# Moving a kernel's row loads behind its first tiles, and its first results into the last product

## The chip, the cores and the metric

The kernel runs on one core of a Trainium2 chip. Its engines are TensorE (PE in the profile), VectorE (DVE), ScalarE (ACT), GpSimd (POOL) and SyncE (SP); DMAs are issued from the queues of SyncE, ScalarE and GpSimd. The metric is the device time of one execution in microseconds, lower is better; of three runs of the kernel before the median counts. Beside them stands one profiled execution.

## The reference

One inference step of a hybrid decoder layer in float32, on 256 prompt tokens and on 8 samples of 8 tokens, 320 tokens in all, of width 2048:

```python
xn = rms_norm(x, g_mix)
z = xn @ w_in                  # [B | C | h | q | k | v | gate_conv | gate_attn]
u = c_gate * h_conv
y_conv = (b_gate * short_conv(u, w_conv)) @ w_conv_out      # causal, width 3
y_attn = window_attention(q, k, v, rel_bias, sinks) @ w_attn_out
merged = sigmoid(gate_c) * y_conv + sigmoid(gate_a) * y_attn
h = x + merged @ w_o
hn = rms_norm(h, g_ffn)
h = h + (silu(hn @ w_gate) * (hn @ w_up)) @ w_down          # inner width 5632
y = rms_norm(h, g_final)       # y_prompt (256 rows), y_sample (64 rows)
```

Returned are y for the prompt and the samples, and the new keys, values and convolution states.

## The kernel before, in words

Every product is computed in pieces of float32r: a loaded weight tile `wraw` is split into a high part `whi` (a copy on ScalarE, line 104) and a low part `wlo` (a subtraction on VectorE, line 105), and for each pair of tiles TensorE runs high by high, low by high and high by low. The rings hold four `wraw`, three `whi` and three `wlo`, so that loads and splits run ahead of TensorE by a few tiles. Weight loads are issued from SyncE's queue. The order of instructions on each engine is fixed when the program is built: a scheduler takes them in program order as far as, by its own model, they are ready; `after(...)` places an instruction behind another one of the same engine.

The start. `vecs` (line 199) holds the norm's weights. x comes in twice: transposed, as `hT` (`x_load`, line 259, the first chunk from ScalarE's queue and the others from SyncE's, six issues among the weight tiles by the table `XA`), and by rows, as `xr` (`row_load`, line 342, six loads from GpSimd's queue). The first product is `kv_product` (line 297) with nine weight tiles: two of one chunk of 128 rows, seven of two chunks. For each tile `x_prep` splits the chunks of `hT` into `xh_t` and `xl_t` (lines 272 and 273, both with `vecs`), then the weights are split and the matmuls of line 316 run, 12 for a chunk. After every tile `tick()` runs one step of the side work `start_rest` (line 349): it builds the bias table through the tile `e_sb`, then issues `row_load` 0 to 2 behind the fifth tile, 3 and 4 behind the sixth, and from the eighth tile on squares one row tile a step on ScalarE (`row_square`, line 347); `row_load(5)` stands behind the first square. The sums of these squares give the norm's root, which enters only when results are taken out of the product. Nothing holds a row load back, so the scheduler may issue it as soon as its buffer is free.

`at_pace` (line 154) is a mark: VectorE copies one element out of the last low part (`last["low"]`) into `marks` (line 157), and GpSimd copies it into `pace` (line 158); what is put behind that copy on GpSimd waits for the tile's split. Before, it is used in later stages alone, and `kv_product` does not set `last["low"]`.

The end. The last product, w_down, is computed by `down(g, ...)` (line 905) for two halves g of the output columns, as a seven-product scheme on sums of blocks; the products come in the order `ORDER`, and the last is `Q4`, of three weight tiles (six matmuls each) in the last piece. After a product `merge` adds the PSUM bank to the rows `hr` (tokens 0 to 127 and 128 to 255) and `done` takes the finished columns' squares (line 1003) into `ssf` and multiplies them by g_final (line 1006). The samples' sums `hs` are folded from two halves of the partitions by `sample_sum` (line 1013: four matmuls into `pz`, a square and a multiplication into `ysm`), which stands before the third tile of each Q4. `before_last` (line 1032), after the last matmul of the last Q4, finishes the first token tile (`finish`: root, two scalings, two stores of 512 KB from SyncE, line 1059) and takes the samples' root (a small matmul into `pzs`, line 1036). Then Q4 is merged into the second token tile (line 903), its last square and root are taken, and lines 1067 to 1081 scale it in four parts of 512 columns with a store each, and scale and store the samples (`ysm`) in two stores.

Of the kernel before, what the change touches and what calls it, by code (L numbers as in the profile page):

```python
# [44 lines left out]
def hybrid_layer(ctx: ExitStack, tc: tile.TileContext, a: dict, o: list):  # L45
# [27 lines left out]
    def after(*marks):  # L73

        es = ExitStack()
        for m in marks:
            es.enter_context(tc.issue_after(m.ins))
        return es
# [6 lines left out]
    def ring_tile(tag, shape, dt):  # L85
        extra = {"wraw": 2, "whi": 1, "wlo": 1}[tag]
        i = turn[tag]
        turn[tag] = (i + 1) % (ring[tag] + (extra if more else 0))
        if i >= ring[tag]:
            return more[0].tile(shape, dt, tag=tag, name=u(tag), bufs=extra)  # L90
        return wp.tile(shape, dt, tag=tag, name=u(tag), bufs=ring[tag])
# [62 lines left out]
    def at_pace():  # L154
        i = paced[0]
        paced[0] += 1
        nc.vector.tensor_copy(marks[:, i:i + 1], last["low"][0:1, 0, 0:1].bitcast(F32))  # L157
        return nc.gpsimd.tensor_copy(pace, marks[:, i:i + 1])  # L158
# [37 lines left out]
                nc.gpsimd.dma_start(flat(block(dst, g, i)), flat(block(src, g, i)))  # L196

    vecs = cst.tile([P, 56], F32, name="vecs")
    nc.gpsimd.dma_start(vecs, a["vecs"])
    ident = cst.tile([P, P], F32, name="ident")  # L200
    nc.gpsimd.memset(ident, 0.0)
    ident_in = nc.gpsimd.affine_select(
# [94 lines left out]
    def kv_product(tiles):  # L297
        ps = [ps_acc(u("kv")) for _ in range(4)]
        k0 = 0
        for i, n in enumerate(tiles):  # L300
            for k in range(k0, k0 + n):
                x_prep(k)
            raw = ring_tile("wraw", [P, 2, CK], F32)
            nc.sync.dma_start(raw[:, :n, :], a["w_kv"][:, k0:k0 + n, :])
            for c0, cn in XA.get(i, ()):
                x_load(c0, cn, nc.sync)
            hi, lo = ring_tile("whi", [P, 2, CK], F32R), ring_tile("wlo", [P, 2, CK], F32R)
            with after(*mark[k0 + n - 1]):
                split_to(hi[:, :n, :], lo[:, :n, :], raw[:, :n, :])
            order = [(k, c) for k in range(n) for c in range(4)]  # L310
            if k0 + n == KC:
                order.sort(key=lambda kc: kc[1])
            for k, c in order:
                kc = k0 + k
                for m, (w, x) in enumerate(((hi, xh), (hi, xl), (lo, xh))):
                    last["mm"] = nc.tensor.matmul(  # L316
                        ps[c][:, :T], w[:, k, c * P:(c + 1) * P], x(kc),
                        start=(kc == 0 and m == 0), stop=(kc == KC - 1 and m == 2),
                    )
            k0 += n  # L320
            tick()
        return ps
# [14 lines left out]
    def row_load(i):  # L337
        t, h = i // 2, i % 2
        t0, tn = TOK[t]
        tag, w = (("s", 1536), ("s", 1536), ("pT", 1536), ("bias", 1024), ("bias", 1024), ("s", 1536))[i]  # L340
        r = pr.tile([P, w], F32, tag=tag, name=u("xr"), bufs=1 if tag == "pT" else 2)
        nc.gpsimd.dma_start(r[:tn, 0:1024], a["x_rows"][t0:t0 + tn, h * 1024:(h + 1) * 1024])
        xr[i] = r[:tn, 0:1024]

    def row_square(i):
# [559 lines left out]
    def down(g, k0, nk, done):  # L905
        sa, al2 = made[0]
        samp = {}
        n1 = slice(g * 2 * SW, (g * 2 + 1) * SW)
        n2 = slice((g * 2 + 1) * SW, (g * 2 + 2) * SW)
        for prods in ORDER:  # L910
            bank = {prod: ps_acc(u(prod)) for prod in prods}
            for prod in prods:
                side = STREAMS[prod][2]
                if side and side not in samp:
                    samp[side] = ps_aux(u("n" + side))
            for i in range(nk // KP):
                if final[0] and prods == ("Q4",) and i == nk // KP - 1:
                    sample_sum(g, n1, n2)
                for prod in prods:
                    name, xv, side = STREAMS[prod]  # L920
                    v = A_OF[prod]
                    hi, lo = load_block(block(name, g, k0 // KP + i), [P, KP, SW])
                    for j in range(KP):
                        kk = i * KP + j
                        first, end = kk == 0, kk == nk - 1
                        xh_, xl_ = a_h[:, v, kk, :], a_l[:, v, kk, :] if v < 5 else al2[:, v - 5, kk, :]
                        for m, (x, w) in enumerate(((xh_, hi), (xl_, hi), (xh_, lo))):
                            last["mm"] = nc.tensor.matmul(  # L928
                                bank[prod], x, w[:, j, :],
                                start=(first and m == 0), stop=(end and m == 2),  # L930
                            )
                        if side:
                            for m, w in enumerate((hi, lo)):
                                last["mm"] = nc.tensor.matmul(  # L934
                                    samp[side], sa[:, xv, kk, :], w[:, j, :],
                                    start=(first and m == 0 and prod == SHARED[side][0]),
                                    stop=(end and m == 1 and prod == SHARED[side][1]),
                                )
                    while pending:
                        with after(last["lo"]):  # L940
                            pending.pop(0)()
                    tick()
            if final[0] and g == 1 and prods == ("Q4",):
                before_last(n2)
            for prod in prods:
                merge(prod, bank[prod], n1, n2)
                done(g, prod, n1, n2)
                side = STREAMS[prod][2]
                if side and prod == SHARED[side][1]:
                    ns = n1 if side == "a" else n2  # L950
                    nc.vector.tensor_add(hs[:, ns], hs[:, ns], samp[side])
                    done(g, "n" + side, n1, n2)
# [10 lines left out]
    for piece, nf in enumerate(PIECES):  # L963
# [41 lines left out]
        def scaled(y, ns):  # L1005
            nc.vector.tensor_mul(y[:, ns], y[:, ns], gfb[:y.shape[0], ns])
# [6 lines left out]
        def sample_sum(g, n1, n2):  # L1013
            pz = ps_aux(u("pz"))
            for h, ns in enumerate((n1, n2)):
                nc.tensor.matmul(
                    pz[h * 64:h * 64 + 64, :], sel[:, 0:64], hs[:, ns], start=True, stop=True
                )
            square(pz, ssf[:, 2, g:g + 1])
            nc.vector.tensor_mul(ysm[:, g, 0:SW], pz, ysm[:, g, SW:2 * SW])  # L1020

        def done(g, prod, n1, n2):
            if not final[0]:
                return
            for p, t, ns in (("P2", 0, n1), ("P7", 1, n2), ("Q3", 0, n2), ("Q4", 1, n1)):
                if p == prod:
                    c = ns.start // SW
                    square(hr[:, t, ns], ssf[:, t, c:c + 1])
                    if g == 0 or p in ("P2", "P7"):
                        scaled(hr[:, t, :], ns)  # L1030

        def before_last(n2):
            scaled(hr[:, 0, :], n2)
            finish(0, hr[:, 0, :], y_p[0, 0:P, :], P, nc.sync)
            pz = ps_aux("pzs")
            nc.tensor.matmul(pz[:, 0:2], sel, ssf[:, 2, 0:2], start=True, stop=True)
            nc.vector.tensor_copy(ssf[:, 2, 0:2], pz[:, 0:2])
            nc.vector.memset(ssf[:, 2, 2:4], 0.0)
            root(2)

        roots = {}

# [21 lines left out]
        side_work[0] = sum_work(2)  # L1064
        f0 += nf

    r = root(1)
    y, dst = hr[:, 1, :], y_p[0, P:TP, :]
    e = slice(2 * SW, 3 * SW)
    nc.vector.scalar_tensor_tensor(y[:, e], y[:, e], r, gfb[:, e], op0=ALU.mult, op1=ALU.mult)  # L1070
    nc.scalar.activation(y[:, 0:SW], y[:, 0:SW], AF.Copy, scale=r)
    nc.sync.dma_start(dst[:, e], y[:, e])
    nc.scalar.dma_start(dst[:, 0:SW], y[:, 0:SW])
    nc.vector.tensor_scalar(y[:, SW:2 * SW], y[:, SW:2 * SW], r, None, op0=ALU.mult)
    nc.vector.tensor_scalar(y[:, 3 * SW:D], y[:, 3 * SW:D], r, None, op0=ALU.mult)
    nc.sync.dma_start(dst[:, SW:2 * SW], y[:, SW:2 * SW])
    nc.scalar.dma_start(dst[:, 3 * SW:D], y[:, 3 * SW:D])
    ys = y_s.flatten_outer_dims().rearrange("t (g h n) -> t h g n", g=2, h=2)
    nc.scalar.activation(ysm[:, :, 0:SW], ysm[:, :, 0:SW], AF.Copy, scale=roots[2])
    for h, eng in ((0, nc.scalar), (1, nc.sync)):  # L1080
        eng.dma_start(ys[:, h], ysm[h * 64:h * 64 + 64, :, 0:SW])


_IN = ['x', 'w_kv', 'w_in', 'w_conv_out', 'w_attn_out', 'w_o', 'w_gate', 'w_up', 'w_down', 'vecs', 'state_conv',
# [84 lines left out]
```

## Time and profile before

| | |
|---|---|
| runs before | 1684.08, 1684.56, 1684.93 us (median 1684.56) |
| profiled execution | 1686.09 us, span 1684.1 us |
| granted TensorE clock | 0.996 mean |
| busy share PE, DVE, ACT, POOL | 99%, 58%, 43%, 12% |
| DMA | 388.31 MB, mean 231 GB/s |

The span reaches from the first to the last instruction of the profiled execution. Busy times are sums over an engine's instructions; an idle engine costs something only where the others wait for it. In the timeline a row has the start, the duration, the engine, the line and the operation, out and in; a trailing q marks the engine's queue, which issues DMAs. In the view by windows a row has the stretch, its length, the busy time of PE, PEld (weight loads of TensorE), DVE, ACT and POOL with the number of instructions, then the granted clock, the mean busy share of the DMA engines and GB/s.

### The profile page before, as it was taken

What the parts mean: (1) busy time and instruction counts of PE and PEld (TensorE: products, weight loads), DVE (VectorE), ACT (ScalarE), POOL (GpSimd) and SP (SyncE); (2) the same over time, 40 slices, a digit from 0 to 9 for tenths busy, and PEclk for the clock granted to TensorE, in tenths of its full rate; (3) what the DMA queues carried; (4) which work ended last, traced back from release to release, by engine and by line L of the source; (5) the groups of instructions that cost most, each with busy time, mean ns of one, the idle gap of its engine ahead of it and who ended that gap; (6) DMA issues with size and microseconds to landing.
All of it is one profiled execution on the core that took longest, in us unless ns stands there. A gap on an engine that the chain in (4) does not pass through costs nothing.

```text
span 1684.1 us, 26855 instructions
## 1 busy us (share of the span) xinstructions
PE 1664.7 (99%) x10692; PEld 1592.6 (95%) x10692; DVE 983.3 (58%) x1544; ACT 724.9 (43%) x934; POOL 200.6 (12%) x449
## 2 busy tenths in 40 slices
PE   8999999999999999999999999999999999999996
PEld 7999999999999999999999988899999888999975
DVE  5457645444444444446555577755555777555686
ACT  6345433333333334445333355433333554333464
POOL 2001211111111112211111100011111000110000
PEclk9999999999999999999999999999999999999998
DMA  9554545888888889997787878888877788787584
GB/s 302 178 145 121 178 137 155 279 256 240 249 246 250 252 252 293 291 282 224 219 225 227 226 244 267 268 251 227 222 225 216 241 274 268 232 233 202 192 280 153
DMA packets 91549, 388.31 MB, mean 231 GB/s; under 512 B 12320, under 2 KB 12640, under 8 KB 84224
## 3 DMA queue, kind: packets, MB, share of 16 engines
q1 hardware_dynamic: 78048, 282.20, 51.5%
q0 software_dynamic: 12800, 103.46, 25.1%
q8 instruction: 83, 1.36, 0.3%
q10 hardware_dynamic: 576, 0.95, 0.2%
q14 instruction: 42, 0.34, 0.1%
HBM read 383.32 MB, written 97.48 MB: 285 GB/s over the span
## 4 chain that ended last, share of the span: by engine, by line
PE 97%; DVE 1%; DMA 1%; ACT 0%; issue 0%; SPq 0%; DVEq 0%; ACTq 0%
PE fu L128 18%; PE fg L128 18%; PE P L928 7%; PE wo L128 7%; PE gc L128 7%; PE ga L128 7%; PE Q L928 5%; PE C L128 3%; PE yc L128 3%; PE ya L128 3%; PE B L128 3%; PE q L128 3%; PE H L128 3%; PE nb L934 2%; PE na L934 2%; PE kv L316 2%
## 5 line engine op out<-in xcount | busy, mean ns | idle before, releaser
L105 DVE TENSOR_TENSOR wlo<-wraw,whi 128x1024 fp32r<-128x1024 f32 (+1 forms) x531 | 650.3, 1225 | 579.1 <-ACT whi L104 576.8
L104 ACT ACTIVATE whi<-wraw 128x1024 fp32r<-128x1024 f32 (+1 forms) x531 | 562.0, 1059 | 790.3 <-PE fu L128 159.0
L128 PE MATMUL fu<-hh_t,whi 128*128 128x320 f32 x704 | 217.9, 309 | 0.0
L128 PE MATMUL fg<-hh_t,whi 128*128 128x320 f32 x704 | 217.8, 309 | 0.0
L128 PE MATMUL fu<-hl_t,whi 128*128 128x320 f32 x704 | 217.8, 309 | 0.0
L128 PE MATMUL fg<-hh_t,wlo 128*128 128x320 f32 x704 | 217.8, 309 | 0.0
L128 PE MATMUL fu<-hh_t,wlo 128*128 128x320 f32 x704 | 217.8, 309 | 0.0
L128 PE MATMUL fg<-hl_t,whi 128*128 128x320 f32 x704 | 217.7, 309 | 0.0
L158 POOL COPY pace<-marks 1x1 f32<-1x1 f32 x180 | 35.4, 196 | 1038.5 <-DVE marks L157 1038.4
L128 PEld LDWEIGHTS fg<-hh_t,whi 128*128 128x128 f32 x704 | 132.3, 188 | 0.1
L128 PEld LDWEIGHTS fg<-hl_t,whi 128*128 128x128 f32 x704 | 132.3, 188 | 0.1
L128 PEld LDWEIGHTS fu<-hh_t,whi 128*128 128x128 f32 x704 | 132.3, 188 | 0.1
L128 PEld LDWEIGHTS fu<-hl_t,whi 128*128 128x128 f32 x704 | 132.3, 188 | 0.0
L128 PEld LDWEIGHTS fu<-hh_t,wlo 128*128 128x128 f32 x704 | 132.3, 188 | 0.0
L128 PEld LDWEIGHTS fg<-hh_t,wlo 128*128 128x128 f32 x704 | 132.3, 188 | 0.0
L128 PE MATMUL wo<-m_h,whi 128*128 128x320 f32 x256 | 79.8, 312 | 0.0
L128 PE MATMUL wo<-m_h,wlo 128*128 128x320 f32 x256 | 79.3, 310 | 0.0
L128 PE MATMUL wo<-m_l,whi 128*128 128x320 f32 x256 | 79.2, 310 | 0.0
L128 PE MATMUL gc<-xh_t,wlo 128*128 128x320 f32 x256 | 79.1, 309 | 0.0
L128 PE MATMUL ga<-xl_t,whi 128*128 128x320 f32 x256 | 79.1, 309 | 0.0
L128 PE MATMUL gc<-xh_t,whi 128*128 128x320 f32 x256 | 79.1, 309 | 0.0
L128 PE MATMUL gc<-xl_t,whi 128*128 128x320 f32 x256 | 79.1, 309 | 0.0
(313 smaller groups left out, 3405.3 us busy)
## 6 DMA issues: line engine op xcount, KB each, us to landing
T<-in_w_down_dram POOLq DMA_DIRECT2D x132, 512.0 KB, 7.1
wraw<-in_w_in_dram SPq DMA_DIRECT2D x128, 512.0 KB, 4.2
wraw<-in_w_gate_dram SPq DMA_DIRECT2D x88, 512.0 KB, 4.7
wraw<-in_w_up_dram SPq DMA_DIRECT2D x88, 512.0 KB, 4.8
wraw<-T SPq DMA_DIRECT2D x88, 512.0 KB, 4.4
wraw<-in_w_down_dram SPq DMA_DIRECT2D x66, 512.0 KB, 4.4
T<-T POOLq DMA_DIRECT2D x44, 512.0 KB, 5.5
wraw<-in_w_o_dram SPq DMA_DIRECT2D x32, 512.0 KB, 6.8
```

The lines of the kernel that those rows point to most:

```text
L104: last["hi"] = nc.scalar.activation(hi, src, AF.Copy)
L105: last["lo"] = nc.vector.tensor_sub(lo, src, hi.bitcast(F32))
L128: last["mm"] = nc.tensor.matmul(ps[c][:, :T], w[:, k, c * P:(c + 1) * P], x(kc), start=(kc == 0 and i == 0), stop=(kc == nk - 1 and i == 2),)
L158: return nc.gpsimd.tensor_copy(pace, marks[:, i:i + 1])
L316: last["mm"] = nc.tensor.matmul(ps[c][:, :T], w[:, k, c * P:(c + 1) * P], x(kc), start=(kc == 0 and m == 0), stop=(kc == KC - 1 and m == 2),)
L928: last["mm"] = nc.tensor.matmul(bank[prod], x, w[:, j, :], start=(first and m == 0), stop=(end and m == 2),)
L934: last["mm"] = nc.tensor.matmul(samp[side], sa[:, xv, kk, :], w[:, j, :], start=(first and m == 0 and prod == SHARED[side][0]), stop=(end ...
```

## The change

- `vecs` is loaded from ScalarE's queue, ahead of x's first chunk, instead of GpSimd's.
- `kv_product` sets `last["low"]`, and every `row_load` is put behind a mark: the loads of rows 0 to 2 behind the low part of the fifth tile, 3 and 4 behind that of the sixth, 5 behind that of the eighth.
- In the last piece `sample_sum` stands before the second tile of Q4 instead of the third. Before the third tile of the last Q4 stand `finish` of the first token tile and `sample_root`, which holds what `before_last` did for the samples, and their scaling and two stores, both from SyncE.
- `scaled` for the first token tile's last columns moves into `done`. `before_last` now sums the three parts of the second tile's squares that are there, divided by the width and with epsilon; after the last square one operation adds the fourth.
- The second token tile is scaled in three operations (columns 1024 to 1535 and 1536 to 2047 on VectorE, 0 to 1023 on ScalarE) and stored in two stores of 512 KB, one from ScalarE and one from SyncE.

```diff
     vecs = cst.tile([P, 56], F32, name="vecs")
-    nc.gpsimd.dma_start(vecs, a["vecs"])
+    nc.scalar.dma_start(vecs, a["vecs"])
...
             hi, lo = ring_tile("whi", [P, 2, CK], F32R), ring_tile("wlo", [P, 2, CK], F32R)
+            last["low"] = lo
...
-        nc.gpsimd.dma_start(r[:tn, 0:1024], a["x_rows"][t0:t0 + tn, h * 1024:(h + 1) * 1024])
+        with after(at_pace()):
+            nc.gpsimd.dma_start(r[:tn, 0:1024], a["x_rows"][t0:t0 + tn, h * 1024:(h + 1) * 1024])
...
             for i in range(nk // KP):
-                if final[0] and prods == ("Q4",) and i == nk // KP - 1:
-                    sample_sum(g, n1, n2)
+                if final[0] and prods == ("Q4",):
+                    if i == 1:
+                        sample_sum(g, n1, n2)
+                    elif g == 1 and i == 2:
+                        finish(0, hr[:, 0, :], y_p[0, 0:P, :], P, nc.sync)
+                        sample_root()
...
-                    if g == 0 or p in ("P2", "P7"):
+                    if g == 0 or p != "Q4":
                         scaled(hr[:, t, :], ns)
-        def before_last(n2):
-            scaled(hr[:, 0, :], n2)
-            finish(0, hr[:, 0, :], y_p[0, 0:P, :], P, nc.sync)
+        def sample_root():
             pz = ps_aux("pzs")
             nc.tensor.matmul(pz[:, 0:2], sel, ssf[:, 2, 0:2], start=True, stop=True)
             nc.vector.tensor_copy(ssf[:, 2, 0:2], pz[:, 0:2])
             nc.vector.memset(ssf[:, 2, 2:4], 0.0)
             root(2)
+            nc.scalar.activation(ysm[:, :, 0:SW], ysm[:, :, 0:SW], AF.Copy, scale=roots[2])
+            ys = y_s.flatten_outer_dims().rearrange("t (g h n) -> t h g n", g=2, h=2)
+            for h in range(2):
+                nc.sync.dma_start(ys[:, h], ysm[h * 64:h * 64 + 64, :, 0:SW])
+        def before_last(n2):
+            c = n2.start // SW
+            nc.vector.memset(ssf[:, 1, c - 1:c], 0.0)
+            s1 = small[:, 29:30]
+            nc.vector.tensor_reduce(s1, ssf[:, 1, :], axis=AX.X, op=ALU.add)
+            nc.vector.tensor_scalar(s1, s1, 1.0 / D, EPS, op0=ALU.mult, op1=ALU.add)
...
-    r = root(1)
+    v1, s, r = (small[:, 30 + i:31 + i] for i in range(3))
+    nc.vector.scalar_tensor_tensor(v1, ssf[:, 1, 2:3], 1.0 / D, small[:, 29:30], op0=ALU.mult, op1=ALU.add)
+    root_steps(v1, s, r, r)
     y, dst = hr[:, 1, :], y_p[0, P:TP, :]
     e = slice(2 * SW, 3 * SW)
     nc.vector.scalar_tensor_tensor(y[:, e], y[:, e], r, gfb[:, e], op0=ALU.mult, op1=ALU.mult)
-    nc.scalar.activation(y[:, 0:SW], y[:, 0:SW], AF.Copy, scale=r)
-    nc.sync.dma_start(dst[:, e], y[:, e])
-    nc.scalar.dma_start(dst[:, 0:SW], y[:, 0:SW])
-    nc.vector.tensor_scalar(y[:, SW:2 * SW], y[:, SW:2 * SW], r, None, op0=ALU.mult)
+    nc.scalar.activation(y[:, 0:2 * SW], y[:, 0:2 * SW], AF.Copy, scale=r)
+    nc.scalar.dma_start(dst[:, 0:2 * SW], y[:, 0:2 * SW])
     nc.vector.tensor_scalar(y[:, 3 * SW:D], y[:, 3 * SW:D], r, None, op0=ALU.mult)
-    nc.sync.dma_start(dst[:, SW:2 * SW], y[:, SW:2 * SW])
-    nc.scalar.dma_start(dst[:, 3 * SW:D], y[:, 3 * SW:D])
-    ys = y_s.flatten_outer_dims().rearrange("t (g h n) -> t h g n", g=2, h=2)
-    nc.scalar.activation(ysm[:, :, 0:SW], ysm[:, :, 0:SW], AF.Copy, scale=roots[2])
-    for h, eng in ((0, nc.scalar), (1, nc.sync)):
-        eng.dma_start(ys[:, h], ysm[h * 64:h * 64 + 64, :, 0:SW])
+    nc.sync.dma_start(dst[:, 2 * SW:D], y[:, 2 * SW:D])
```

## The prediction

> **What bounds the kernel now.** I read the page's busy times first, then the waits of TensorE, then the timeline of the only two places where TensorE stands still: the first 17 us and the last 14.
>
> ```profile
> span 1684.1 us, 26855 instructions
> ...
> PE 1664.7 (99%) x10692; PEld 1592.6 (95%) x10692; DVE 983.3 (58%) x1544; ACT 724.9 (43%) x934; POOL 200.6 (12%) x449
> ```
>
> TensorE is busy for 1664.7 of 1684.1 us, so only the other 19.4 us, and time at a low clock, are open to a change that leaves its matmuls alone. The waits of TensorE name one large one:
>
> ```profile
> PE kv L316 <- ACT whi L104: 3.6, 2, 3.4
> ...
> PE q L128 <- DVE qs L678: 0.7, 1, 0.7
> ```
>
> The timeline shows it (start, duration, engine, line; in brackets the idle time before and its releaser):
>
> ```profile
> 1.28 0.72 POOL L199 DMA_DIRECT2D vecs<-in_vecs_dram  x1 [0.82 <-POOLq L1156]
> ...
> 2.13 0.56 POOL L342 DMA_DIRECT2D xr<-in_x_rows_dram  x1
> ...
> 2.61 0.43 SPq L304 DMA_DIRECT2D wraw<-in_w_kv_dram  x1
> ...
> 4.76 0.56 ACT L272 ACTIVATE xh_t<-hT,vecs 128x320 fp32r<-128x320 f32 x1 [2.06 <-DMA vecs<-in_vecs_dram]
> ...
> 6.18 0.61 POOL L342 DMA_DIRECT2D xr<-in_x_rows_dram  x1
> ...
> 9.80 0.31 PE L316 MATMUL kv<-xh_t,wlo 128*128 128x320 f32 x1
> ...
> 12.37 1.06 ACT L104 ACTIVATE whi<-wraw 128x1024 fp32r<-128x1024 f32 x1 [1.76 <-DMA wraw<-in_w_kv_dram]
> ...
> 13.48 0.64 PE L316 MATMUL kv<-xh_t,whi 128*128 128x320 f32 x1 [3.37 <-ACT whi L104]
> ...
> 40.09 0.31 PE L316 MATMUL kv<-xh_t,wlo 128*128 128x320 f32 x1
> ```
>
> The second tile's last matmul starts at 9.80; the third tile's weights, issued at 2.61, land only at 12.35, and TensorE goes on at 13.48. Matmuls of this product start 0.147 us apart (192 of them; the last starts at 40.09), so 13.48 - 9.95 = 3.5 us are lost. Meanwhile two loads of x's rows (2.13 and 6.18), which no work of this stretch reads, share the DMA engines. The same stretch by windows (busy times, then the granted clock, DMA share, GB/s):
>
> ```profile
> 0.00:5.00 5.00, 3.37 (x8) 1.19 (x9) 0.67 (x3) 1.73 (x3) 3.85 (x12) 1.00 0.68 190
> 5.00:10.00 5.00, 4.76 (x26) 3.73 (x24) 2.28 (x4) 2.21 (x5) 1.80 (x4) 1.00 0.99 286
> 10.00:13.40 3.40, 0.11 (x1) 0.00 (x0) 1.02 (x2) 1.64 (x3) 0.54 (x1) 0.98 0.91 350
> 13.40:14.00 0.60, 0.52 (x2) 0.52 (x3) 0.54 (x1) 0.25 (x2) 0.00 (x0) 0.50 1.03 416
> ...
> 16.00:17.00 1.00, 1.00 (x6) 1.00 (x6) 0.00 (x0) 0.58 (x1) 0.00 (x0) 0.68 1.05 418
> ...
> 20.00:25.00 5.00, 5.00 (x35) 4.78 (x35) 4.58 (x9) 4.56 (x9) 1.57 (x3) 1.00 1.02 399
> ```
>
> After the wait the clock is 0.50 from 13.40 to 16.00 and 0.68 in the next us: 2.6 x 0.50 + 1.0 x 0.32 = 1.6 us more. The start thus loses 5.1 us.
>
> **Part 1, the rows behind the marks.** How much of the 5.1 us comes back depends on when the third tile lands without the rows. Sizes and times to landing, from the DMA view of the first 45 us:
>
> ```profile
> wraw<-in_w_kv_dram SPq DMA_DIRECT2D x7, 512.0 KB, 10.2
> ...
> xr<-in_x_rows_dram POOLq DMA_DIRECT2D x4, 512.0 KB, 7.9
> ...
> hT<-in_x_dram SPq DMA_DIRECT2D x3, 320.0 KB, 10.7
> wraw<-in_w_kv_dram SPq DMA_DIRECT2D x2, 256.0 KB, 3.5
> ...
> hT<-in_x_dram ACTq DMA_DIRECT2D x1, 160.0 KB, 3.5
> ```
>
> Up to that tile SyncE's queue carries 2 x 256 + 160 + 320 + 512 KB; with x's first chunk (160 KB) and some 120 KB of constants (by the code's shapes) that is 1.83 MB. By the windows 0.95 MB have moved at 5 us, and at 286 GB/s the other 0.88 MB take 3.1 us more: 8.1. A landing lags the last byte: of the 4.0 us that line 1059's 1 MB takes below, its bytes at 399 GB/s are 2.6, which leaves 1.4 for both ends, and half of that, 0.7, behind. So 8.8 at best. The constants no longer stand behind the rows in POOL's queue and drain earlier, in front of this tile; I put the landing at 9.3. TensorE follows a landing by 13.48 - 12.35 = 1.13 us: 10.4, a wait of 0.5 us instead of 3.5, and I take the clock to stay up, since after 9.95 it went low only in the last 0.1 us before 13.40 (0.98 over 3.40 us). Gain 3.0 + 1.6 = **4.6 us**. Ends: 5.1, the whole loss; below, if the 1.05 MB of rows had slowed the tile by half their bytes only (0.52 MB at 286 GB/s, 1.8 us) and the clock fell all the same, 1.8 us. I stay near the upper end, because the rows make up nearly all of what moved before 12.35 beyond the 1.83 MB (0.95 + 1.43 + 1.75 x 0.35 = 2.99 MB by 11.75).
>
> By the Trainium skill (TensorE: Matmul & The Clock Gate, "Part 1: The HAM clock gate") the array drops to half clock after about one idle window of 3.4 us, on a window that runs freely; the drop about 3.4 us after 9.95 agrees. By it a wait of 0.5 us costs no clock and the gain is 4.6; were every wait to cool the array, it would be 3.0.
>
> What the move makes late: each of the six loads now waits on POOL for a copy, which waits for a one-element copy on VectorE behind the low part of the fifth, sixth or eighth tile. The cost per copy on POOL, and the first user of the rows:
>
> ```profile
> L158 POOL COPY pace<-marks 1x1 f32<-1x1 f32 x180 | 35.4, 196 | 1038.5 <-DVE marks L157 1038.4
> ```
>
> ```profile
> 27.42 1.04 ACT L347 ACTIVATE xr<-xr 128x1024 f32<-128x1024 f32 x1
> ```
>
> Six such copies on POOL are 1.2 us, which only the row loads and the attention's bias loads behind them see; the six on VectorE, of one element too, are as short and lie in its idle time, since a two-chunk tile is 24 x 0.147 = 3.52 us of TensorE. With the third tile starting at 10.4, the fifth starts at 17.4 and its low part is made between 14 and 17.5. POOL's queue also holds the write of e_sb ahead; so the first row load goes out at 15 to 19 and lands after 7.9 us, at 23 to 27. The high parts have three buffers, so the eighth waits for the fifth tile's end at 21.3; ScalarE squares the first row behind it, at about 22.5, and a late row holds the ninth tile's split, which TensorE wants at 31.9: split and low part take 1.06 + 1.2 us and the square 1.2, so a row may land until 28.4 without a stall. The cover is 1.4 us at its thinnest; every us beyond costs one. Cost taken 0, upper end 1.5. SyncE's weights then share the engines with the rows from 15 to 30, where the measured 399 GB/s stand against 852 KB per 3.52 us (242 GB/s): cost 0.
>
> **vecs on ScalarE's queue.** One issue of about 0.4 us goes in front of x's first chunk and before ScalarE's table load, and 0.72 us leaves POOL, whose constants go out earlier. The first split, held by vecs until 4.76, is then held by x's chunk, issued at 1.2, landing 3.5 later at 4.7: 0, ends -0.3 and +0.3.
>
> **Part 2, the tail.** The rows from the last product on:
>
> ```profile
> 1665.84 0.68 DVE L951 TENSOR_TENSOR hs<-hs,nb 128x512 f32<-128x512 f32 x1
> ...
> 1668.22 1.08 PE L1016 MATMUL pz<-hs,ones 128*64 128x512 f32 x4
> ...
> 1670.50 0.39 PE L928 MATMUL Q<-wlo,a_h 128*128 128x512 f32 x1
> 1670.50 0.42 PEld L1036 LDWEIGHTS pzs<-rbsq,ones 128*128 128x128 f32 x2
> ...
> 1670.76 0.74 DVE L1056 TENSOR_SCALAR hr<-hr,rbsq 128x1024 f32<-128x1024 f32 x1
> ...
> 1671.48 0.68 DVE L903 TENSOR_TENSOR hr<-hr,Q 128x512 f32<-128x512 f32 x1
> ...
> 1672.26 0.63 ACT L1003 ACTIVATE gt<-hr 128x512 f32<-128x512 f32 x1 [1.10 <-DVE rbsq L1046]
> ...
> 1673.88 1.15 ACT L1079 ACTIVATE gt<-gt,rbsq 128x1024 f32<-128x1024 f32 x1 [0.29 <-DVE rbsq L228]
> ...
> 1674.41 0.75 DVE L1070 SCALAR_TENSOR_TENSOR hr<-hr,rbsq,gt 128x512 f32<-128x512 f32 x1
> ...
> 1675.47 0.48 DVE L1075 TENSOR_SCALAR hr<-hr,rbsq 128x512 f32<-128x512 f32 x1
> ...
> 1677.02 1.97 ACTq L1077 DMA_DIRECT2D out_dram<-hr  x1
> ```
>
> - The merge L903 could start at 1670.95, when the last matmul is through, but VectorE is at the first tile's scaling until 1671.50. In the changed kernel that work, and the sample's sums one block (1.4 us) earlier, are over by then. Against it stand the small matmul L1036, which can now fall inside the product (0.42), and hs, ready at 1666.52, just when the sum wants it. Gain 0.2, ends -0.1 and 0.5.
> - The last root loses one of its small steps: from the square's end (1672.26 + 0.63) to 1674.41 eight of them take 1.52, 0.19 each. The three steps that now add up the other parts (some 0.6) are ready before the last block ends and lie under it. Gain 0.2.
> - From root to scaled rows: 1674.41 to 1675.95 now; L1070 and L1075 alone are 1.2, and ScalarE's half, one operation of L1079's shape, is 1.15. Gain 0.3.
> - From scaled rows to landing. The last store (line 1077) and the first tile's two (line 1059) to landing, min/median/max:
>
> ```profile
> DMA to landing us min/median/max: 5.8/5.8/5.8
> ```
>
> ```profile
> 1671.19 0.81 SPq L1059 DMA_DIRECT2D out_dram<-hr  x2
> ```
>
> ```profile
> DMA to landing us min/median/max: 2.7/3.1/3.6
> ```
>
> Now the last landing is 1677.02 + 5.8 = 1682.8, or 6.9 after the rows are ready: six stores, 1.5 MB, share it. Afterwards two stores of 512 KB go out at once on two queues. Line 1059 did those 1 MB in 4.0 us (second issue about 1671.6, plus 3.6). Gain 2.9, if the sample's 0.5 MB, now behind line 1079's operation one block earlier, are through; else 1.3 less (at 399 GB/s). Both of its stores now issue from SyncE (0.4 each by line 1059) ahead of the last one, which they hold up only in that case.
> - The sample's scaling (1.15) used to run after the last square; in ScalarE's order it may now stand in front of the last square or root: 0 to 1.15 lost, I take 0.5.
>
> Sum 0.2 + 0.2 + 0.3 + 2.9 - 0.5 = **3.1 us**, ends 0.6 (store 1.3 less, 1.15 lost, merge -0.1) and 3.6.
>
> **Sum.** 4.6 + 3.1 = 7.7. Between the two ends TensorE paces everything and its waits elsewhere are 0.7 and less, so the early gain reaches the end whole. The profiled execution took 1686.09 (span 1684.1), 1.53 above the median of 1684.56; it would become 1678.4 with a span of 1676.4, and the median **1676.9**. What such a kernel's measurement tells from no change is 0.2%, 3.4 us.
>
> **The rivals.**
> 1. The rows come back as a wait (slower). For it: they only move, into 15 to 30 us, and ScalarE takes them in order. The Trainium skill (DMA: Bandwidth & Descriptors, "Issuing engines are not separate DMA queues") says transfers of all queues run on the same 16 engines and interleave. Against it: the margins above and 399 GB/s at full demand. To eat 7.7 + 3.4 us a row would have to land at 28.4 + 11.1 = 39.5, over 20 us after its issue, where 7.9 was measured. At that point the time is 1688. Chance 0.04.
> 2. The third tile is late for the constants too, not only for the rows, and 1.8 us is all that the start gives: 1684.56 - 1.8 - 3.1 = 1679.7. For it: 286 GB/s in 5 to 10 us, well under 399, with small transfers about. Chance 0.15.
> 3. The tail gives little, because the sample's scaling and stores collide with the last root and stores: 4.6 + 0.6, 1679.4. For it: ScalarE has the sample's square, two scalings of 1.15 and two roots between the sums and the last square. Chance 0.15.
> 4. Both 2 and 3: 2.4 us, 1682.2, no change. Chance 0.06.
>
> **How the numbers follow.** My forecast has 0.60, its own range 1675.5 to 1678.6 (gains of 8.7 and 0.4 for the scatter of the runs, down to a start of 3.6 and a tail of 2.4). Rivals 2 and 3 lie at 1679 to 1680; the range 1675.2 to 1680.8 takes them in and leaves out rivals 1, 4 and their neighbours. Faster: 0.60 + 0.15 + 0.15 less 0.03 for the slow ends of 2 and 3, 0.87; same 0.09; slower 0.04.
>
> **What would show it.** TensorE's wait for the high part in the first 17 us under 1 us, no window at 0.5 before the tail, the last kv matmul near 35.7 instead of 40.1; row loads first issued after 15 and no ScalarE wait for them that TensorE feels; the merge by 1671.3 less the early gain; two stores after the last root, landing about 4 us after issue. Wrong if TensorE waits near 32 us for a split, if the third tile lands after 11, or if the sample's stores go out after the last root.

## The result, and the profile after

| | median | runs | lowest to highest |
|---|---|---|---|
| before (beside these runs) | 1684.76 us | 19 | 1684.08 to 1685.41 |
| after | 1681.49 us | 19 | 1680.44 to 1682.22 |

The ratio is 0.998, 95% interval 0.9973 to 0.9987: 3.3 us less (2.2 to 4.5), against a forecast of 7.7 and a range that ended at 1680.8. The profiled execution after took 1681.36 us. The page:

```profile
span 1679.6 us, 26868 instructions
...
PE 1663.7 (99%) x10692; PEld 1591.4 (95%) x10692; DVE 983.9 (59%) x1551; ACT 725.1 (43%) x934; POOL 206.5 (12%) x454
```

The span is 4.5 us shorter. Three numbers of the two timelines divide it: the last matmul of the key/value product starts at 36.04 instead of 40.09 (4.05), the last Q matmul at 1666.77 instead of 1670.50 (3.73), and from there to the end it is 12.8 us instead of 13.6 (0.8). So 0.3 of the start's gain is lost again in between.

The start after, by its timeline:

```profile
4.55 0.56 ACT L272 ACTIVATE xh_t<-hT,vecs 128x320 fp32r<-128x320 f32 x1 [1.38 <-DMA hT<-in_x_dram]
...
9.73 1.06 ACT L104 ACTIVATE whi<-wraw 128x1024 fp32r<-128x1024 f32 x1 [0.35 <-DMA wraw<-in_w_kv_dram]
...
10.84 0.41 PE L317 MATMUL kv<-xh_t,whi 128*128 128x320 f32 x1 [0.69 <-ACT whi L104]
...
17.18 3.08 POOL L158 COPY pace<-marks 1x1 f32<-1x1 f32 x1 [1.02 <-DVE marks L157]
20.21 0.57 POOL L344 DMA_DIRECT2D xr<-in_x_rows_dram  x1
...
26.82 1.06 ACT L349 ACTIVATE xr<-xr 128x1024 f32<-128x1024 f32 x1 [3.60 <-DMA xr<-in_x_rows_dram]
...
35.20 1.06 ACT L349 ACTIVATE xr<-xr 128x1024 f32<-128x1024 f32 x1 [1.42 <-DMA xr<-in_x_rows_dram]
...
36.04 0.31 PE L317 MATMUL kv<-xh_t,wlo 128*128 128x320 f32 x1
```

The third tile's split begins at 9.73 (12.37 before) and TensorE goes on at 10.84 (13.48 before). The clock stays up, in the view by windows:

```profile
5.00:10.00 5.00, 4.96 (x26) 4.21 (x24) 3.29 (x6) 2.89 (x7) 0.00 (x0) 1.00 0.95 271
10.00:13.40 3.40, 2.71 (x19) 2.48 (x18) 2.48 (x5) 2.98 (x5) 2.41 (x2) 1.00 1.04 407
13.40:16.00 2.60, 2.60 (x18) 2.19 (x18) 2.60 (x6) 2.02 (x4) 0.36 (x1) 1.00 1.02 412
```

The tail after, last product to last store (SPq and ACTq are the queues that issue the stores):

```profile
1666.77 0.40 PE L934 MATMUL Q<-wlo,a_h 128*128 128x512 f32 x1
1667.21 0.69 DVE L905 TENSOR_TENSOR hr<-hr,Q 128x512 f32<-128x512 f32 x1 [0.41 <-PE Q L934]
...
1669.63 1.15 ACT L1044 ACTIVATE gt<-gt,rbsq 128x1024 f32<-128x1024 f32 x1 [0.49 <-DVE rbsq L228]
...
1670.68 1.13 ACT L1088 ACTIVATE hr<-hr,rbsq 128x1024 f32<-128x1024 f32 x1
1670.81 1.26 SPq L1047 DMA_DIRECT2D out_dram<-gt  x2
1671.85 0.36 ACTq L1089 DMA_DIRECT2D out_dram<-hr  x1
1672.16 0.62 SPq L1091 DMA_DIRECT2D out_dram<-hr  x1
```

And the stores of the last us in the DMA view (queue, size, us from issue to landing):

```profile
out_dram<-gt SPq DMA_DIRECT2D x2, 256.0 KB, 4.1
out_dram<-hr ACTq DMA_DIRECT2D x1, 512.0 KB, 4.9
out_dram<-hr SPq DMA_DIRECT2D x1, 512.0 KB, 5.9
```

The merge waits for TensorE alone, as forecast. But the sample's scaling (line 1044, tile `gt`) starts at 1669.63, 0.3 before the last root is there (1669.92, where VectorE's last step ends), and holds ScalarE until 1670.7. The sample's two stores go out at 1670.81, after the last root, and stand on SyncE's queue in front of the last store. That one is issued at 1672.16, though VectorE has its rows ready at 1671.10, and lands 5.9 later, at 1678.1.

### The profile page after: what moved, and what is told of

The parts are those of the page before. It is cut to its first block, busy times and chain, and to the rows that moved or that the text cites. A ratio compares the mean times of both kernels' runs of the same rounds, so it can differ in the third digit from the quotient of the medians.

```text
span 1679.6 us, 26868 instructions
## 1 busy us (share of the span) xinstructions
PE 1663.7 (99%) x10692; PEld 1591.4 (95%) x10692; DVE 983.9 (59%) x1551; ACT 725.1 (43%) x934; POOL 206.5 (12%) x454
## 4 chain that ended last, share of the span: by engine, by line
PE 98%; DVE 1%; ACT 0%; DMA 0%; issue 0%; SPq 0%
PE fu L128 18%; PE fg L128 18%; PE P L934 7%; PE wo L128 7%; PE ga L128 7%; PE gc L128 7%; PE Q L934 6%; PE C L128 3%; PE ya L128 3%; PE yc L128 3%; PE B L128 3%; PE q L128 3%; PE H L128 3%; PE na L940 2%; PE nb L940 2%; PE kv L317 1%
## 5 line engine op out<-in xcount | busy, mean ns | idle before, releaser
L158 POOL COPY pace<-marks 1x1 f32<-1x1 f32 x186 | 41.2, 222 | 1038.9 <-DVE marks L157 1038.9
L128 PE MATMUL ga<-xh_t,whi 128*128 128x320 f32 x256 | 79.2, 309 | 0.0
```

The costliest lines, as they stand in the source:

```text
L128: last["mm"] = nc.tensor.matmul(ps[c][:, :T], w[:, k, c * P:(c + 1) * P], x(kc), start=(kc == 0 and i == 0), stop=(kc == nk - 1 and i == 2),)
```

## The experiments

The kernel before had medians of 1684.69, 1684.79 and 1684.81 us beside the three groups of runs. "Gain" is against that median of its own group. Positions are those of the one profiled execution of each kernel, in us: where TensorE goes on with the third tile, the last key/value matmul, the last Q matmul, the end of the span.

| kernel | median | ratio, 95% interval | gain | third tile | last kv | last Q | end |
|---|---|---|---|---|---|---|---|
| before_again | 1684.78 | 0.9991 to 1.0009 | -0.1 | 12.82 | 39.47 | 1669.22 | 1682.8 |
| start_only | 1682.11 | 0.9976 to 0.9993 | 2.6 | 11.10 | 36.29 | 1666.05 | 1679.5 |
| tail_only | 1683.75 | 0.9985 to 1.0003 | 0.9 | 13.11 | 40.85 | 1670.82 | 1682.8 |
| sample_first | 1679.78 | 0.9959 to 0.9982 | 4.9 | 11.54 | 36.74 | 1666.95 | 1678.0 |
| warm_gap | 1684.30 | 0.9987 to 1.0005 | 0.5 | 13.30 | 39.40 | 1669.15 | 1682.7 |
| no_sample | 1677.88 | 0.9945 to 0.9972 | 6.9 | 11.61 | 36.82 | 1666.94 | 1676.4 |
| vecs_pool | 1680.83 | 0.9967 to 0.9985 | 4.0 | no wait | 35.25 | 1666.94 | 1679.3 |
| tile_first | 1678.67 | 0.9951 to 0.9976 | 6.1 | 11.72 | 36.92 | 1667.68 | 1677.3 |
| after_again | 1681.29 | 0.9969 to 0.9987 | 3.5 | 11.79 | 36.99 | 1666.94 | 1679.7 |
| vecs_pool_again | 1680.62 | 0.9965 to 0.9984 | 4.2 | 12.05 | 38.70 | 1668.67 | 1681.0 |
| rows_fourth | 1681.64 | 0.9969 to 0.9987 | 3.2 | 10.86 | 36.05 | 1667.22 | 1680.0 |
| best | 1677.54 | 0.9945 to 0.9970 | 7.3 | 10.38 | 35.85 | 1666.38 | 1675.8 |

**The two parts alone.** before_again is the kernel before, unaltered, for a second trace. start_only has the `vecs` line, `last["low"]` and the marks, with the old tail; tail_only has all the rest, with the old start.

> The kernel before, unchanged, with its own span and clock in every run. Theory A: the profiled execution of before (1686.09, 1.5 over its median) holds a fall to half clock of 1.6 us behind the 3.5 us wait that an ordinary run does not have. Then most runs have a span near 1682.5 and a mean clock of 0.997 or more, and only single ones reach 1684 with 0.996. Rival A': every run has the fall; all spans lie near 1684 with 0.996, and the 1.5 us are elsewhere.

> Part 1 alone: vecs from ScalarE's queue and the row loads behind marks, with the old tail. The profiles show the start 3.85 us shorter, 1.6 of it the clock. Theory A (ordinary runs of before keep the clock): 2.3 us faster than before, near 1682.4. Rival A' (they lose it too): 3.8 us faster, near 1680.9, and then the tail part must have cost 0.6. Prediction on record: 4.6 faster.

> Part 2 alone: the new tail on the old start. Theory A: 0.9 us faster than before, near 1683.8 (the profiles: last landing 4.74 earlier, of it 3.85 from the start). Rival A': 0.5 slower, near 1685.2. Prediction on record: 3.1 faster.

The sizes add up: 2.6 + 0.9 = 3.5, and the whole change gave 3.3 and 3.5. (tail_only's interval holds zero.) Both parts fell short. Theory A's numbers were met, but its reason falls: the fall of the clock was not peculiar to one execution. before_again and tail_only have it too (0.50 in the window 13.40 to 16.00, as the first profile). What differs from one execution to the next is when TensorE gets the third tile, 13.48, 12.82 and 13.11 with the old start, and how long the clock stays low: by windows of 1 us until about 16.7 in the first profile and in before_again, until 18.9 in tail_only.

**Is the clock a cost of its own?** warm_gap adds to the kernel before, behind the second key/value tile:

```diff
+            if i == 1:
+                wm2 = ps_aux("wm2")
+                for _ in range(8):
+                    with after(last["mm"]):
+                        last["mm"] = nc.tensor.matmul(wm2, busy[:, :P], busy, start=True, stop=True)
```

> The kernel before, with eight products of 512 columns on constant data put behind the second key/value tile, into the wait for the third; nothing else. Theory (the fall to half clock from 13.4 us is what the long wait leaves behind, and it costs ordinary runs too): the granted clock stays 1.00 from 10 to 20 us, and the time falls by about 1.6, to 1683.1. Rival (the clock is not a cost of its own: the first products after the wait are limited by something else, or ordinary runs do not lose it): 1684.7, no change. If the eight products run at the slow spacing (0.43 each, 3.4 us together) they end about when the third tile is ready, so they cannot cost more than 0.3.

```profile
10.23 1.90 PE L325 MATMUL wm<-busy 128*128 128x512 bf16 x8
13.30 0.41 PE L316 MATMUL kv<-xh_t,whi 128*128 128x320 f32 x1 [1.16 <-ACT whi L104]
...
14.56 0.41 PE L316 MATMUL kv<-xh_t,wlo 128*128 128x320 f32 x1 [0.70 <-DVE wlo L105]
```

The eight products keep the clock at 1.00 in every window from 10 to 20 us, but the gain is 0.5, not 1.6, and the interval holds zero. That does not settle it, because the edit also changed the order of TensorE's work. In the kernel before, the third tile's eight matmuls with the high part come first and the four with the low part behind them:

```profile
15.78 1.15 PE L316 MATMUL kv<-xh_t,wlo 128*128 128x320 f32 x4
```

In the changed kernel it is the same order:

```profile
12.12 0.83 PE L317 MATMUL kv<-xh_t,wlo 128*128 128x320 f32 x4
```

In warm_gap a matmul with the low part stands third, while VectorE makes that part from 13.28 to 14.51, and TensorE loses 0.9 there (13.70 to 14.56). The changed kernel, at full clock too, has the low part at 12.05, in time for 12.12. So this wait is the experiment's own. From the third tile to the last kv matmul warm_gap takes 26.1; less the 0.9 it would be 25.2, an estimate, and 25.2 is what seven traces of the new start with a high clock took. The old start takes 26.6, 26.65 and, with the longer fall of tail_only, 27.7. One trace of the new start in which the clock fell (vecs_pool_again, below) takes 26.65. So a fall of some 3.4 us costs 1.4, near the 1.6 that theory and prediction gave it; as a time without a trace this is not shown.

**The sample in front of the last rows.** sample_first takes the sample's root between the halves of Q4's second tile, scales the sample before the last square and puts one half of the first token tile's scaling behind the last merge; the table that the root's first step needs is loaded earlier:

```diff
                     if i == 1:
                         sample_sum(g, n1, n2)
-                    elif g == 1 and i == 2:
-                        finish(0, hr[:, 0, :], y_p[0, 0:P, :], P, nc.sync)
-                        sample_root()
+                        if g == 1:
+                            sample_root()
+                            first_tile(1)
...
-                done(g, prod, n1, n2)
+                with after(*([last["ysc"]] if late else [])):
+                    done(g, prod, n1, n2)
+                if late:
+                    with after(last["mrg"]):
+                        first_tile(0)
```

> The changed kernel, with the sample's root matmul forced between the two halves of the second block of the last product, the sample's scaling forced before the last square, half of the first tile's scaling behind the last merge, and the root's table load taken out of the tail. Theory B: the tail's gain was eaten because the sample's scaling (1.15 us) stands in front of the last scaling on ScalarE and its stores (0.5 MB) in front of the last store on SyncE's queue; taken out of the way, the two last stores land about 3.6 us after their issue instead of 5.9, and the kernel takes 2.7 us less than the changed one, near 1678.8. Rival B': two stores side by side to memory take 5 to 6 us by themselves; then at most the 0.75 us of ScalarE's wait come back, near 1680.7.

```profile
1668.10 1.26 SPq L1055 DMA_DIRECT2D out_dram<-gt  x2
1669.46 0.62 SPq L1081 DMA_DIRECT2D out_dram<-hr  x1
1671.31 0.34 SPq L1098 DMA_DIRECT2D out_dram<-hr  x1
```

It gained 1.7 on the changed kernel's first runs, between theory and rival. Both last stores now go out together, at 1671.31, but land 5.0 and 5.5 later, because a store of the first token tile (1669.46) and the sample's are still draining. no_sample asks what the sample costs in all:

```diff
-            nc.scalar.activation(ysm[:, :, 0:SW], ysm[:, :, 0:SW], AF.Copy, scale=roots[2])
...
-            for h in range(2):
-                nc.sync.dma_start(ys[:, h], ysm[h * 64:h * 64 + 64, :, 0:SW])
+            nc.sync.dma_start(ys[:, 0, 0:1, 0:2], ysm[0:64, 0:1, 0:2])
```

> The changed kernel without the scaling of the sample's result and without its two stores (0.5 MB; only a few elements are sent); the sample's output is left out, all sums and roots stay. Theory (the sample's scaling stands in front of the last scaling on ScalarE, its stores in front of the last stores): last scaling starts when the root is ready (0.8 earlier), the last stores are issued at about 0.75 to 1.0 earlier and land 4.0 after issue instead of 4.9 and 5.9: gain 2.9, 1678.6. Rival (two stores of 0.5 MB take 5 to 6 us whatever stands before them): 0.75 to 1.0 alone, 1680.6.

```profile
out_dram<-hr SPq DMA_DIRECT2D x1, 512.0 KB, 3.8
out_dram<-hr ACTq DMA_DIRECT2D x1, 512.0 KB, 3.9
```

The two last stores, on an empty path, land 3.8 and 3.9 after their issue at 1671.30, which is 4.4 after the last Q matmul (5.4 in the changed kernel). From the last Q matmul to the end it is 9.5 us instead of 12.8: the sample's scaling and stores cost the changed kernel 3.4 in the traces, 3.6 in the medians. The rival, that such stores take 5 to 6 by themselves, is out. tile_first keeps the sample and gives it room: both halves of the first token tile right behind their root, the sample's multiplication while its root's first step runs.

```diff
-                        sample_sum(g, n1, n2)
-                        if g == 1:
-                            sample_root()
-                            first_tile(1)
+                        if g == 1:
+                            first_tile(1)
+                            first_tile(0)
+                        sample_sum(g, n1, n2)
+                        if g == 1:
+                            sample_root()
```

> The kernel with the sample's root put between the halves of Q4's second block, and in it both halves of the first token tile scaled and sent right behind its root (before: one half behind the last merge), the sample's multiplication between its variance and its root. Theory (what stands in the queues when the last stores are issued sets their landing): the last scaling starts 0.25 later, but 0.5 MB less stands in front, so that the last stores land 4.3 instead of 5.0 and 5.5 after issue: 1679.0, 0.8 below the 1679.8 of the kernel without this. Rival (the two stores of the sample, with rows of 2 KB, are what drains slowly, or the stores themselves take over 5): 1680.0.

```profile
out_dram<-gt SPq DMA_DIRECT2D x2, 256.0 KB, 3.2
out_dram<-hr SPq DMA_DIRECT2D x1, 512.0 KB, 3.8
out_dram<-hr ACTq DMA_DIRECT2D x1, 512.0 KB, 4.0
```

3.8 and 4.0 again, with the sample's stores issued 3.0 before the last two. They land at about 1672.3 and 1673.0, after the issue of the last two (1672.15), but nearly all bytes are through by 1672.5, before those of the last two come (DMA share 0.24, then 1.02 in the next us):

```profile
1672.50:1673.00 0.50, 0.00 (x0) 0.00 (x0) 0.00 (x0) 0.00 (x0) 0.00 (x0) 1.00 0.24 86
```

The tail is 9.6 us, and 1678.67 is 1.1 below sample_first. The theory holds: bytes still to be moved in front of the last stores made 3.9 into 5.9.

**What the start still waits for.** after_again and vecs_pool_again ran on the same chip; vecs_pool has one line changed, `nc.gpsimd.dma_start(vecs, ...)`. rows_fourth moves the first row loads one tile up:

```diff
         yield
-        yield
         for i in range(3):
             row_load(i)
+        yield
         nc.gpsimd.dma_start(
             bias_s, ...
```

> The changed kernel once more, unaltered, to stand beside the next one on the same chip: 1681.5, as before. In its trace TensorE is to wait 0.7 to 1.5 for the third key/value tile, whose split starts at 9.7 to 10.6, as in the four other traces with the small vector load on ScalarE's queue.

> The changed kernel with the small vector load back on GpSimd's queue. Theory: 1681.5 within 0.3 either way. Rival (it takes 0.3 from the loads that ScalarE's first work waits for, or frees GpSimd for the row loads): 1680.9 or 1682.1.

> The changed kernel with the small vector load back on GpSimd's queue, once more, beside the changed kernel itself. In its first trace the third tile's split began at 8.03 with no wait, and 1.2 went again at 35.7 to 36.9, where TensorE waited for the copy that frees a bank of the key/value product, behind the squares of the late rows. Theory (the place of that load decides whether the third tile or a piece of x lands first): split at about 8 again, 0.7 below the changed kernel, 1680.8. Rival (chance in the landing of the third tile; both kernels are the same): within 0.3 of the changed kernel, split anywhere from 8 to 10.6.

> The changed kernel with the first five row loads one tile earlier, behind marks of the fourth tile. Theory (the rows come back as a wait of ScalarE, 3.60 for the first and 1.42 for the fourth, and TensorE feels of it only what is left after the key/value product, 0.2 in the changed kernel's trace): ScalarE's wait falls by 2 or more, the time by 0.2, 1681.3. Rival (2.5 MB one tile earlier take the rate from the sixth and seventh weight tiles, as they did from the third before the change): TensorE waits for weights between 14 and 25 us, 0.5 to 1.5 slower, 1682.5.

vecs_pool was 0.66 and vecs_pool_again 0.67 below the changed kernel, but the intervals overlap and its runs scatter from 1679.28 to 1682.81: that the moved load costs 0.7 is suggested, not shown. The theory that the load's place decides whether the third tile lands first came near in time (1680.62 for 1680.8), but by luck: the split began at 8.03 in one trace and at 10.95 in the other. The two traces show what scatters. In vecs_pool the third tile's split began at 8.03 and TensorE met no wait, then this at the product's end:

```profile
35.69 0.31 PE L128 MATMUL q<-xh_t,wlo 128*128 128x320 f32 x1
36.91 0.41 PE L128 MATMUL q<-xh_t,whi 128*128 128x320 f32 x1 [0.90 <-ACT kT L388]
```

TensorE wants the bank that ScalarE's copy `kT` frees, and the copy stands behind the square of a late row (35.38, which had waited 2.39 for its load): 1.1 of the earlier tile is given back. In vecs_pool_again the split began at 10.95, TensorE stood still from 10.1 to 12.05, and the clock fell after this wait of 1.9 us:

```profile
13.00:14.00 1.00, 1.00 (x5) 1.00 (x5) 0.98 (x4) 0.54 (x1) 0.00 (x0) 0.50 1.04 424
```

after_again waited as long (9.9 to 11.79, more than the 0.7 to 1.5 expected) and kept its clock. So with the third tile at 9.7 to 11 the new start is still near the edge. With `vecs` on ScalarE's queue the clock fell in none of seven traces; how often it does in runs without a trace is open. start_only gives a hint: its two slowest runs of eleven (1683.47 and 1683.56) have a mean clock of 0.996, as vecs_pool_again's trace has, the others 0.997 or 0.998.

rows_fourth gained nothing, and the rows of GpSimd and VectorE in its timeline say why:

```profile
15.29 0.25 DVE L157 COPY marks<-wlo 1x1 f32<-1x1 f32 x3
...
16.16 4.01 POOL L158 COPY pace<-marks 1x1 f32<-1x1 f32 x1
...
17.07 1.92 DVE L273 SCALAR_TENSOR_TENSOR xl_t<-hT,vecs,xh_t 128x320 fp32r<-128x320 f32 x4
...
18.92 1.21 DVE L105 TENSOR_TENSOR wlo<-wraw,whi 128x1024 fp32r<-128x1024 f32 x1
...
20.11 0.57 POOL L344 DMA_DIRECT2D xr<-in_x_rows_dram  x1
```

The marks are there 1.7 earlier than in the changed kernel (15.29 against 16.98), but GpSimd's copy of one element now takes 4.01 instead of 3.08 and the first row load leaves at 20.11 instead of 20.21. Neither expectation foresaw this.

**Together.** best is tile_first with the rows one tile up and `vecs` on GpSimd.

> The kernel with the early sample's root and both halves of the first token tile behind their root (1678.7), with the rows one tile earlier and the small vector load back on GpSimd. If both of these do what the first theories say, third tile without wait (1.2 less) and no wait at the end of the key/value product: 1677.4. Rival (neither is worth anything): 1678.7.

1677.54, 3.75 below the changed kernel on the same chip and 7.3 below the one before. That is near the first theories' 1677.4, but its trace does not bear their reasons out: TensorE still stood still from 10.0 to 10.38 for the third tile and lost 0.3 at the product's end, and the first row load left at 20.50. What the last two edits add to tile_first (1.1, five runs each in different groups) is not separated from scatter.

## Why the prediction was wrong

The direction was right, both mechanisms were there, and both terms were too large. The outcome, 1681.5, lies nearest to rival 4 (1682.2), which the prediction gave 0.06. Two steps failed: the landing of the third tile, and the landing of the last stores.

- **Third tile, forecast 3.0 of wait gone.** The first step that failed, on both ends. The landing was put at 9.3; with `vecs` where the change puts it, the split began at 9.73 to 10.68 in seven traces, and TensorE went on at 10.84 to 11.79, mean 11.35. "The other 0.88 MB take 3.1 us more" lets only what stands in front of the third tile, and the tile itself, move before its landing. But in the changed kernel SyncE's queue (q1) had moved 1.69 MB by 9.0 (the prediction's lag of 0.7 before the landing at 9.7) and 1.94 by 9.7, and the queue up to and with the tile holds 1.54: loads issued behind it move along with it. GpSimd's queue is q0 (packets, MB, share of the DMA engines' time):

```profile
q1 hardware_dynamic: 777, 1.69, 54.5%
q0 software_dynamic: 109, 0.03, 13.4%
```

In the kernel before, up to 11.65 (again 0.7 before the landing), 2.84 MB had moved, and of them:

```profile
q1 hardware_dynamic: 865, 1.94, 51.7%
q0 software_dynamic: 366, 0.74, 26.6%
```

GpSimd's 0.74 MB contain 0.12 of constants. So the rows were some 0.6 of the 1.0 MB beyond the prediction's 1.83, not "nearly all"; the other 0.4 came from SyncE's own later loads, and those the change leaves where they are. Whether the small constants slow the tile too, as rival 2 had it, is open: they took 13.4% of the DMA engines' time to 9.0 us, and no run left them out. And the loss of the one profile was taken for typical: in three traces of the old start TensorE went on at 12.82 to 13.48, mean 13.14. 13.14 - 11.35 = 1.8.

- **Clock, forecast 1.6.** The size is about right: from the third tile to the end of the product 26.65 with a fall of the clock and 25.2 without, 1.4. By the Trainium skill (TensorE: Matmul & The Clock Gate, "Part 1: The HAM clock gate") the array cools after an idle window of about 3.4 us. The traces differ: it cooled after a wait of 1.9 us in vecs_pool_again, and some 2.1 us into the wait of tail_only.
- **Late rows, forecast 0.** The first row landed at 26.8, inside the cover until 28.4, and no split came late. But the copy that frees the product's bank was not on the list of what stands behind the squares: it cost TensorE 0.2 in the changed kernel's trace, 1.1 in vecs_pool and rows_fourth. Issue at 15 to 19 became 20.2, because a one-element copy was costed at its mean of 196 ns.
- **vecs, forecast 0.** The first split is held by x's chunk, as forecast (4.55). Whether the move has a price, some 0.7 by the medians of vecs_pool, stays open.
- Together 1.8 + 1.4 - 0.2 = 3.0 in the traces, tail_only's longer fall left aside; start_only measured 2.6 (1.2 to 4.0).
- **Merge, root and scaled rows, forecast 0.7 less 0.5.** From the last Q matmul to the rows scaled it is 5.04 instead of 5.45: 0.4, near the 0.2 forecast. Moving the small matmul `pzs` into the product costs TensorE 0.2 (from the last kv to the last Q matmul 1629.75 in before_again and warm_gap, 1629.95 in after_again).
- **Scaled rows to landing, forecast 2.9.** This is the second step that failed: 6.9 became 6.2, not 4.0. The 4.0 itself was right (3.8 to 4.0 in no_sample, tile_first and best), but its condition, "if the sample's 0.5 MB are through", was not met, and rival 3 named why: the sample's scaling held up the last one on ScalarE by 0.76 (1670.68 instead of 1669.92), and its stores stood in front of the last. The named sign of error, the sample's stores after the last root, is the row at 1670.81. The sum's 0.5 priced ScalarE alone. The bytes were priced at 1.3, at 399 GB/s, and the two issues at 0.4 each, and both were left out of the sum; the issues took 1.26, and the sample's stores moved at about 200 GB/s (last section), so that 0.52 MB are 2.6 us, an estimate.
- **From the profile to the median.** The forecast took the whole gain from the median, although the profiled execution stood 1.53 above it. Of that, before_again shows 0.6 at the third tile (12.82 against 13.48) and 0.7 between the key/value product and the last Q matmul, which no run here explains. A loss that only this execution had can't be won back in the others.

## What to carry to other kernels

Work moved off the end helps only if the bytes of its stores are through before those of the last stores come: for each moved store write down issue time, queue position, rate and landing against the last one's issue. When you work out when a load lands, count the loads issued behind it as well. A loss read in one trace is one sample; take a second trace of the same kernel before subtracting it from a median. When a wait shrinks, list everything that stands behind the late work on its engine, the copies that free a bank too. When an experiment adds work, compare the order of the instructions before and after: in warm_gap the added products moved a matmul ahead, and the wait behind it hid most of what was to be measured.

## What was not expected of the hardware

A GpSimd copy of one element took 0.17 to 0.20 us mostly, but 3.08 and 1.74 (changed kernel) and 4.01 (rows_fourth) while VectorE ran two-input operations back to back (3.00 of 3.00 us busy from 17 to 20), and ended in both within 0.1 of VectorE's next one-element copies, at 20.2. By the Trainium skill (SBUF — State Buffer, "Who interferes with whom") a VectorE instruction with two SBUF inputs contends with a GpSimd instruction that reads SBUF, and the loser blocks for that whole instruction. The rows agree and go further: here it stayed blocked over five such instructions in a row in the changed kernel (four of line 273, one of line 105). That the shared port is the cause was not tried by itself.

While the sample's stores drained (rows of 2 KB, 64 partitions each), the DMA engines moved 203 GB/s at a busy share of 0.94 (1672 to 1674 in the changed kernel), and 383 at 0.96 in the same two us of no_sample with 4-KB rows from 128 partitions. In tile_first, where the sample's stores were alone from 1670.5 to 1672.0, it was 184 to 213. Whether the rows' length or the number of partitions sets this rate, no run here separates.
